# Gate pieces moved between groups, another order of products in a projection, and a last block gated before it is stored

## The chip, the core and the metric

The kernel runs on one core of one Trainium2 chip. Its engines are TensorE (PE in the profile, with PEld for its weight loads), VectorE (DVE), ScalarE (ACT), GpSimd (POOL) and SyncE (SP); transfers run on 16 DMA engines, issued by the queues of SP, POOL and ACT. The metric is the time of one execution on the device in microseconds, as the median of several runs.

## What is computed

One block of a diffusion model over 512 latent tokens and 256 context tokens with 2048 channels, all in fp32:

```python
shift, scale, gate = split(silu(c) @ w_ada + b_ada, 3)          # the same with c_ctx for the context
h  = rmsnorm(x, norm_g) * (1 + scale) + shift                   # hc for the context
p  = h @ w_in                                                   # q, k, v, z_a, u_b, z_b, g_a, g_b: 9216 columns
kc, vc = columns k, v of hc @ w_in
attn = attention(rope(rmsnorm(q)), [rope(rmsnorm(k)), rmsnorm(kc)], [v, vc])   # 12 query heads, 4 key heads
y_a = (attn * silu(z_a)) @ w_proj_a
y_b = (fft2(u_b).real * silu(z_b)) @ w_proj_b
y   = (sigmoid(g_a) * y_a + sigmoid(g_b) * y_b) @ w_out
out = rmsnorm(x + gate * y, final_g)
```

## The kernel before

**Products.** The large projections are computed in groups. A group makes a block of 512 tokens by 1024 or 512 columns with a Strassen-Winograd scheme in seven products, in the order P1, Q5, P2, Q6, P7, Q3, Q4 (`ONE_GROUP`), P1, P2, Q5, Q6, P7, Q3, Q4 (`OUT_GROUP`) for the branch and output projections. A product takes four pieces of weights (three in branch A), each 128x1024. A piece is multiplied in three passes (lines 322 to 324), since each fp32 factor is split into a high and a low part: ACT writes the high part of a piece (`whi`, line 173; `s` where it is split in halves), DVE the low part (`wlo`, line 174). PE needs both.

**Weights.** SP loads pieces in the order of use into a few raw buffers (`wr`, line 209), and a load waits until DVE has used what was in its buffer before. Some products need sums and differences of weight pieces. These are made in four chain tiles (`R`, numbers 1303 to 1306), which SP loads first, by accumulating loads on POOL's queue (line 277) or additions on DVE (line 256); P7's pieces are differences on DVE (line 262).

**Groups.** Groups 0 to 2 make the queries, 3 and 4 and later 6 and 7 the two gates g_a and g_b, and group 5 keys and values, for the context as well (`KV`). The modulated context is made from its rows beside groups 3 and 4. Then come 48 attention steps (12 heads in four blocks of queries), filled up with branch B's projection; then two groups of branch A's projection (10 and 11); then two groups of the output projection. `after(n, ...)` puts work off by n turns.

**The output gate.** `gate` is a product of one row with a matrix, and DVE makes it. The matrix comes in 32 pieces of 512 KB (`w_gate`), and `use_gate` (line 1091) multiplies each with half of the condition row (`crow`, loaded in two halves by `load_row`; `silu_of_row`, lines 1081 and 1082, turns a half into its silu in place) and sums it. `GATE_AT` tells behind which piece of which product a gate piece is used: 28 of them in the groups, the rest in the attention steps. A gate piece takes a raw buffer like a weight piece, from its load until DVE has used it.

**Merging.** Branch B's part of y is stored in `yb_d`. When a block of branch A's projection is finished, `branch_done` multiplies it with its gate on DVE (line 1357), adds `yb_d` to it by an accumulating transfer on POOL's queue (line 1359), and has it transposed by PE (line 1368) some turns later; the output projection's factors are made from the transposes.

Of the kernel before, what the change touches and what calls it, by code (L numbers as in the profile page):

```python
# [18 lines left out]
P = 128  # L19
# [38 lines left out]
OUT_GROUP = ("P1", "P2", "Q5", "Q6", "P7", "Q3", "Q4")  # L58

# [12 lines left out]
def context_piece(g, name, pc):  # L72
# [4 lines left out]
    if n % 6 == 0 and 18 <= n < 42:  # L77
# [39 lines left out]
def block_kernel(ctx, tc, xT, ctx_rows, ctx_toks, x, c_row, w_ss, w_gate, vecs, qkg, rope, dft_c, dft_s,  # L117
# [676 lines left out]
    class Group:  # L794
# [16 lines left out]
        def steps(self, name):  # L811
# [12 lines left out]
            for pc in range(self.pieces):  # L824
# [20 lines left out]
                if q is not None:  # L845
                    use_gate(q, get(("gate", q)))
                    if q == KK - 1:
                        raw_pools.append((rp, 1, "raw0", 1))
# [225 lines left out]
    def load_row(half):  # L1074
        row = crow[half] = rp.tile([P, 1024], F32, tag=f"raw{half}", bufs=1, name=uid("crow"))
# [47 lines left out]
    for g, kind in enumerate(KINDS):  # L1123
        if g == 3:
            jobs += [lambda: None] * 8 + [context_norm, lambda: None, lambda: None, context_spread]
# [11 lines left out]
        for name in ONE_GROUP:  # L1137
            if (g, name) in ((0, "Q4"), (KV + 1, "P1")):
                assert not any(p[2] == "raw0" for e in ahead for p, _ in e.raws) or g
# [3 lines left out]
            elif (g, name) == (KV + 1, "P2"):  # L1143
# [16 lines left out]
            elif (g, name) == (KV + 1, "Q6"):  # L1160
                raw_pools.append((gvp, 2, "raw", 2))
# [118 lines left out]
    def values(half):  # L1280
# [40 lines left out]
        if second and h == NH - 1:  # L1321
            branch_forms(2)
# [7 lines left out]
    def branch_forms(q):  # L1330
# [3 lines left out]
        branch_form("S3", q, u[:, :, lo])  # L1334
        nc.vector.tensor_tensor(u[:, :, hi], u[:, :, hi], v[:, :, hi], op=ALU.subtract)
        branch_form("Z5", q, u[:, :, hi])
        nc.vector.tensor_tensor(u[:, :, lo], u[:, :, lo], v[:, :, hi], op=ALU.add)
        branch_form("S2", q, u[:, :, lo])
        nc.vector.tensor_tensor(v[:, :, lo], v[:, :, lo], u[:, :, lo], op=ALU.subtract)
        give(u)  # L1340
        branch_form("S4", q, v[:, :, lo])
        give(v)
# [407 lines left out]
```

## Time and profile before

| | us |
|---|---|
| runs | 1353.55, 1360.97, 1353.3 |
| median | 1353.55 |
| the profiled execution | 1350.64 |
| its span on the core | 1348.6 |
| PE busy | 1296.9 |
| DVE busy | 995.4 |
| ACT busy | 683.5 |
| POOL busy | 179.5 |

The rows in the prediction are from this one profiled execution, so sums are made against 1350.64, and the median is 2.9 us above it. A row of stretches has the borders and length in us, then busy time and number of instructions of PE, PEld, DVE, ACT and POOL, the granted clock of PE as a share of full speed, the share of time in which the DMA engines were busy, and GB/s. A row of a timeline has its start and length, the engine and line, the operation, what it writes and reads, and in brackets how long the engine had been idle before it and what released it. A row of waits has the engine and line that waited, what it waited for, and the total, the number and the longest in us. Line numbers are those of the kernel before; the changed file's are larger by two in the first part and by seven further on.

### The profile page before, as it was taken

To read this page: it belongs to the slowest core of one execution; us is meant where nothing else is said; L and a number is where in the kernel's file an instruction comes from. 1 tells how busy PE (TensorE), PEld (TensorE's weight loads), DVE (VectorE), ACT (ScalarE), POOL (GpSimd) and SP (SyncE) were. 2 spreads that over 40 slices of the span, in tenths; PEclk is the share of its full clock that TensorE was granted. 3 is DMA by queue.
4 is the path that set the end of the run, shared out by engine and by line. 5 is a ranking of instruction groups with operands and counts; after the bars stand their busy time and mean duration, and the time that the engine had idled before them with its cause. 6 is when DMAs were issued, how large, how long until landed. Compare 5 with 4: busy or idle time off the path is not lost.

```text
span 1348.6 us, 17538 instructions
## 1 busy us (share of the span) xinstructions
PE 1296.9 (96%) x6522; PEld 1057.5 (78%) x6522; DVE 995.4 (74%) x1294; ACT 683.5 (51%) x1079; POOL 179.5 (13%) x244
## 2 busy tenths in 40 slices
PE   7999999999998999999989999889999999999997
PEld 3676888888886888888867877778888778878885
DVE  4666899889677778747567858667777767778776
ACT  5222655655454544444244534556677545555544
POOL 0110011111101011011021111111100202121210
PEclk9999999999998999999999999889999999999998
DMA  9898587888887999878669888965440799988986
GB/s 385 338 375 306 200 216 226 246 231 233 219 304 196 294 270 266 291 170 221 224 169 316 287 250 283 301 200 166 164 136 17 215 240 223 266 182 221 216 213 174
DMA packets 103718, 318.54 MB, mean 236 GB/s; under 512 B 9808, under 2 KB 33104, under 8 KB 99280
## 3 DMA queue, kind: packets, MB, share of 16 engines
q0 software_dynamic: 30288, 123.75, 38.8%
q1 hardware_dynamic: 48720, 163.65, 34.2%
q10 hardware_dynamic: 24624, 30.02, 6.4%
q8 instruction: 51, 0.84, 0.2%
q14 instruction: 35, 0.29, 0.1%
HBM read 283.30 MB, written 34.09 MB: 235 GB/s over the span
## 4 chain that ended last, share of the span: by engine, by line
PE 57%; DMA 15%; DVE 13%; issue 11%; ACT 4%; POOL 1%; ACTq 0%; DVEq 0%; SPq 0%; POOLq 0%
PE banks L322 8%; PE banks L324 7%; PE banks L323 7%; PE x L323 4%; PE x L324 4%; PE x L322 4%; DVE wlo L174 4%; DMA wr<-in_w_g 4%; PE y L323 4%; PE y L324 3%; PE y L322 3%; PE pd L521 2%; DVE s L174 2%; DMA cf_d<-qr 2%; PE pb L322 2%
## 5 line engine op out<-in xcount | busy, mean ns | idle before, releaser
L173 ACT ACTIVATE whi<-R 128x1024 fp32r<-128x1024 f32 x138 | 144.8, 1057 | 146.6 <-PE banks L324 48.9
L174 DVE TENSOR_TENSOR wlo<-R,whi 128x1024 fp32r<-128x1024 f32 x138 | 167.6, 1222 | 63.6 <-ACT whi L173 63.2
L173 ACT ACTIVATE whi<-wr 128x1024 fp32r<-128x1024 f32 (+1 forms) x123 | 128.4, 1050 | 138.3 <-PE banks L324 34.4
L174 DVE TENSOR_TENSOR wlo<-wr,whi 128x1024 fp32r<-128x1024 f32 (+1 forms) x123 | 148.8, 1214 | 57.8 <-ACT whi L173 57.4
L322 PE MATMUL banks<-whi,s 128*128 128x512 f32 x396 | 158.3, 400 | 7.2 <-DVE ev L849 5.8
L323 PE MATMUL banks<-wlo,s 128*128 128x512 f32 x396 | 156.6, 395 | 0.7 <-DVE wlo L174 0.7
L324 PE MATMUL banks<-whi,s 128*128 128x512 f32 x396 | 156.5, 395 | 0.0
L323 PE MATMUL x<-wlo,s 128*128 128x512 f32 x352 | 138.1, 392 | 4.9 <-DVE wlo L174 4.9
L324 PE MATMUL x<-whi,s 128*128 128x512 f32 x352 | 138.0, 392 | 0.0
L322 PE MATMUL x<-whi,s 128*128 128x512 f32 x352 | 137.9, 392 | 0.0
L323 PE MATMUL y<-wlo,s 128*128 128x512 f32 x316 | 123.2, 390 | 0.8 <-DVE wlo L174 0.8
L322 PE MATMUL y<-whi,s 128*128 128x512 f32 x316 | 123.2, 390 | 0.4 <-DVE cxe L992 0.4
L324 PE MATMUL y<-whi,s 128*128 128x512 f32 x316 | 122.8, 389 | 0.0
L277 POOL DMA_DIRECT2D R<-in_w_g x64 | 55.4, 866 | 451.1 <-DVE wlo L174 207.7
L173 ACT ACTIVATE s<-wr 128x512 fp32r<-128x512 f32 (+2 forms) x93 | 60.2, 676 | 66.6 <-DMA wr<-in_w_g 23.0
L322 PEld LDWEIGHTS banks<-whi,s 128*128 128x128 f32 x396 | 75.6, 191 | 23.3 <-issue 6.2
L324 PEld LDWEIGHTS banks<-whi,s 128*128 128x128 f32 x396 | 75.3, 190 | 15.8
L323 PEld LDWEIGHTS banks<-wlo,s 128*128 128x128 f32 x396 | 75.5, 191 | 15.6 <-DVE wlo L174 1.1
L174 DVE TENSOR_TENSOR s<-wr,s 128x512 fp32r<-128x512 f32 (+2 forms) x93 | 67.1, 752 | 23.3 <-ACT s L173 22.4
L323 PEld LDWEIGHTS x<-wlo,s 128*128 128x128 f32 x352 | 66.6, 189 | 19.1 <-DVE wlo L174 5.5
L324 PEld LDWEIGHTS x<-whi,s 128*128 128x128 f32 x352 | 66.7, 189 | 13.8
L322 PEld LDWEIGHTS x<-whi,s 128*128 128x128 f32 x352 | 66.5, 189 | 13.9
(288 smaller groups left out, 2846.2 us busy)
## 6 DMA issues: line engine op xcount, KB each, us to landing
wr<-in_w_g SPq DMA_DIRECT2D x128, 512.0 KB, 4.8
R<-in_w_g POOLq DMA_DIRECT2D x64, 512.0 KB, 6.9
wa<-in_w_ss POOLq DMA_DIRECT2D x26, 1024.0 KB, 8.2
R<-in_w_g SPq DMA_DIRECT2D x32, 512.0 KB, 5.3
wr<-in_w_gate SPq DMA_DIRECT2D x32, 512.0 KB, 4.9
wr<-in_w_o SPq DMA_DIRECT2D x24, 512.0 KB, 7.5
R<-in_w_o POOLq DMA_DIRECT2D x24, 512.0 KB, 8.3
wr<-in_w_pab SPq DMA_DIRECT2D x20, 512.0 KB, 5.4
```

The source lines that it names most:

```text
L173: first = nc.scalar.activation(hi, src, ACT.Copy)
L174: return first, nc.vector.tensor_tensor(lo, src, hi.bitcast(F32), op=ALU.subtract)
L277: nc.gpsimd.dma_start(chain[e.pc], e.nxt, accum_op=ALU.add)
L322: nc.tensor.matmul(o, ah, bh, start=start, stop=False, skip_group_check=cont)
L323: nc.tensor.matmul(o, ah, bl, start=False, stop=False, skip_group_check=cont)
L324: nc.tensor.matmul(o, al, bh, start=False, stop=stop, skip_group_check=cont)
L521: last = nc.tensor.matmul(acc[32 * j : 32 * j + 32, :256], c2[:, 8 * h + k, :], w[:, k, :], start=n < 4, stop=n >= KK - 4)
```

## The change

Several parts are changed together:

- **Gate pieces.** `GATE_AT` now has nine gate pieces in the K/V group (six before), five in group 6 and five in group 7 (six and eight before), and none in group 4 (one before). The six that are left are used in attention steps 8 to 33, every fifth step, where four were used in steps 4 to 22, every sixth.
- **The second half of the condition row** goes into the other buffer, `raw0`, is loaded earlier, and becomes silu one product earlier, at Q5 of group 6. The buffer `raw1` goes back to the weights in group 6 and `raw0` in the attention steps.
- **Context.** `context_norm` and `context_spread` stand two jobs later.
- **Branch A's products** come in the order P1, P2, Q5, P7, Q6, Q3, Q4, and the block that P7 finishes is finished at Q6.
- **Weight sums** of branch A are made in steps 8 to 25 (3 to 20 before).
- **Forms of branch A** (sums of blocks of its input, and their splits) are made one at a time in steps 43 to 49 instead of by fours at two steps and the end.
- **The last block** of branch A is gated in two parts. `less_gated` multiplies -Y by the gate and adds `yb_d` to it by the accumulating transfer before the last product, Q4; after Q4 `branch_done` multiplies the product with the gate and adds the two in SBUF, and has the block transposed after three turns instead of six.

```diff
+BRANCH_GROUP = ("P1", "P2", "Q5", "P7", "Q6", "Q3", "Q4")
...
-GATE_AT = ([(g, n, 1) for g in (1, 2) for n in ("P2", "Q6", "Q3")] + [(3, "Q5", 1), (4, "P2", 1)]
-           + [(5, n, 1) for n in ("P1", "P2", "Q6", "P7", "Q3", "Q4")] + [(6, n, 1) for n in ONE_GROUP if n != "Q5"]
-           + [(7, n, 1) for n in ONE_GROUP] + [(7, "Q6", 3)])
+GATE_AT = ([(g, n, 1) for g in (1, 2) for n in ("P2", "Q6", "Q3")] + [(3, "Q5", 1)]
+           + [(5, "P1", 1), (5, "Q5", 1), (5, "P2", 1), (5, "Q6", 1), (5, "P7", 1), (5, "P7", 3), (5, "Q3", 1),
+              (5, "Q3", 3), (5, "Q4", 0)] + [(6, n, 1) for n in ("P2", "Q6", "P7", "Q3", "Q4")]
+           + [(7, n, 1) for n in ("P1", "Q5", "P2", "Q6", "P7")])
...
-        for name in OUT_GROUP:
+        for name in BRANCH_GROUP:
             stream_product(name, BRANCH_A + n, BranchWeights(n), (), 3)
...
                 sub(self.Y, self.V, self.Y)
+                if self.g >= BRANCH_A:
+                    sub(self.V, self.V, self.acc["c"])
+                    self.done(1, 1, self.V, self.V)
+            elif name == "P7" and self.g >= BRANCH_A:
+                pass
...
+            elif name == "Q4" and self.g == BRANCH_A + 1:
+                self.done(1, 0, a, self.Y)
...
-        row = crow[half] = rp.tile([P, 1024], F32, tag=f"raw{half}", bufs=1, name=uid("crow"))
+        row = crow[half] = rp.tile([P, 1024], F32, tag="raw0", bufs=1, name=uid("crow"))
...
-            jobs += [lambda: None] * 8 + [context_norm, lambda: None, lambda: None, context_spread]
+            jobs += [lambda: None] * 10 + [context_norm, lambda: None, lambda: None, context_spread]
...
-            elif (g, name) == (KV + 1, "P2"):
+            elif (g, name) == (KV + 1, "Q5"):
                 silu_of_row(1, gvp.tile([P, 1024], F32, tag="raw", bufs=2, name=uid("e")))
...
-                raw_pools.append((gvp, 2, "raw", 2))
+                raw_pools += [(rp, 1, "raw1", 1), (gvp, 2, "raw", 2)]
...
+        if n and (half, c) == (1, 0):
+            nc.vector.tensor_tensor(w, v, w, op=ALU.mult)
+            nc.vector.tensor_tensor(t, t, w, op=ALU.add)
+            give(w)
+            merged[j, half] = t
+            after(3, lambda: turn_merged(j, half))
+            return
...
+    def less_gated(y, j):
+
+        nc.vector.scalar_tensor_tensor(y, y, -1.0, ga[1, j], op0=ALU.mult, op1=ALU.mult)
+        nc.gpsimd.dma_start(flat(y), yb_d[1, j], accum_op=ALU.add)
...
-        if 3 <= i < 21:
-            n, step = divmod(i - 3, 3)
+        if 8 <= i < 26:
+            n, step = divmod(i - 8, 3)
...
-        if 2 <= i < 26 and i % 6 in (2, 4):
-            n, last = NGATE + (i - 2) // 6, i % 6 == 4
+        if 5 <= i < 35 and i % 5 in (0, 3):
+            n, last = NGATE + (i - 5) // 5, i % 5 == 3
...
-        if i in (43, 47):
-            branch_forms(i > 43)
+        for q, name in {43: [(0, "Z5"), (0, "S3")], 44: [(0, "S2")], 45: [(0, "S4")], 47: [(1, "Z5")], 48: [(1, "S3")],
+                        49: [(1, "S2"), (1, "S4")]}.get(i, ()):
+            branch_forms(q, name)
...
+            if name == "Q6" and n:
+                load_ga(1, A_CHUNKS[n][0])
+            elif name == "Q3" and n:
+                after(1, lambda: less_gated(group.Y, A_CHUNKS[n][0]))
```

**ACT around the second half of the condition row**, in group 6. `qr` holds keys that line 966 stores into `k_d`; `e` is the helper of the row's silu and lies where `qr` lay; whi and s are high parts of weight pieces. Before:

```order
L966 DMA k_d<-qr 128x4x128 x2
L173 ACTIVATE whi_5472<-R_1306 128x1024
L173 ACTIVATE whi_5491<-wr_5489 128x1024
L173 ACTIVATE whi_5509<-wr_5507 128x1024
L1081 ACTIVATE e_5541<-crow_5386 128x1024
L173 ACTIVATE s_233<-wr_5544 128x2x256
L173 ACTIVATE s_346<-wr_5544 128x2x256
L857 COPY ev_5539<-y_5470 128x1024
```

Now (its lines 973, 175 and 1088 are those of 966, 173 and 1081):

```order
L175 ACTIVATE whi_5478<-R_1306 128x1024
L175 ACTIVATE whi_5497<-wr_5495 128x1024
L175 ACTIVATE whi_5515<-wr_5513 128x1024
L973 DMA k_d<-qr 128x4x128 x2
L175 ACTIVATE s_233<-wr_5547 128x2x256
L175 ACTIVATE s_346<-wr_5547 128x2x256
L1088 ACTIVATE e_5473<-crow_5392 128x1024
L175 ACTIVATE s_494<-wr_5565 128x2x256
L175 ACTIVATE s_610<-wr_5565 128x2x256
```

The store of the keys has moved behind three splits, and the splits of one more piece (two halves) have moved ahead of `e`.

**SP's loads from the end of the gate groups into the attention steps.** `in_w_g` are weights of the gates, `in_w_gate` pieces of the output gate, `k_d` and `v_d` keys and values, `b_d` tables of the Fourier mixing, `in_w_pab` weights of branches A and B. Before:

```order
L209 DMA wr_6296<-in_w_g 128x1024
L209 DMA wr_6367<-v_d 128x768
L209 DMA wr_6370<-in_w_gate 128x1024
L209 DMA wr_6403<-b_d 128x1024
L209 DMA wr_6416<-b_d 128x1024
L209 DMA wr_6426<-in_w_pab 128x1024
L209 DMA wr_6471<-k_d 128x768
L209 DMA wr_6523<-v_d 128x768
L209 DMA wr_6448<-in_w_pab 128x1024
```

Now:

```order
L211 DMA wr_6296<-k_d 128x768
L211 DMA wr_6449<-k_d 128x768
L211 DMA wr_6314<-v_d 128x768
L211 DMA wr_6379<-b_d 128x1024
L211 DMA wr_6400<-b_d 128x1024
L211 DMA wr_6413<-in_w_pab 128x1024
L211 DMA wr_6423<-in_w_pab 128x1024
L211 DMA wr_6517<-v_d 128x768
```

The gate piece is gone, and the second piece of branch B's weights stands directly behind the first, ahead of the second load of values; the second load of keys has moved ahead.

**DVE at P7 of the last gate group.** Line 262 (264 now) makes the difference of a chain tile and a loaded piece, line 1091 (1098 now) uses a gate piece. Before:

```order
L262 TENSOR_TENSOR wr_6165<-R_1304,wr_6165 128x1024
L174 TENSOR_TENSOR wlo_6168<-R_1305,whi_6167 128x1024
L174 TENSOR_TENSOR wlo_6186<-R_1306,whi_6185 128x1024
L1091 TENSOR_SCALAR wr_6091,gparts<-wr_6091,crow_5386 128x1024
L174 TENSOR_TENSOR wlo_6208<-wr_6148,whi_6207 128x1024
L262 TENSOR_TENSOR wr_6204<-R_1306,wr_6204 128x1024
L174 TENSOR_TENSOR s_234<-wr_6165,s_233 128x2x256
```

Now, some ten instructions earlier:

```order
L1098 TENSOR_SCALAR wr_5935,gparts<-wr_5935,crow_5392 128x1024
L264 TENSOR_TENSOR wr_6204<-R_1306,wr_6204 128x1024
L176 TENSOR_TENSOR wlo_6065<-wr_6000,whi_6064 128x1024
L176 TENSOR_TENSOR wlo_6097<-wr_6055,whi_6096 128x1024
L264 TENSOR_TENSOR wr_6133<-R_1303,wr_6133 128x1024
```

The difference with chain tile 1306, the last one before, has become the first of the four.

More of the change, by code (lines that the diff above doesn't have):

```diff
@@ L1138, in block_kernel @@
             if (g, name) in ((0, "Q4"), (KV + 1, "P1")):
-                assert not any(p[2] == "raw0" for e in ahead for p, _ in e.raws) or g
+                assert not any(p[2] == "raw0" for e in ahead for p, _ in e.raws)
                 load_row(int(g > 0))
@@ L1321, in values @@
         if second and h == NH - 1:
-            branch_forms(2)
+            for name in FORM_ORDER:
+                branch_forms(2, name)
     def branch_form(name, q, src):
@@ L1483, in block_kernel @@
     for n, group in enumerate(a_groups):
[L1484 to L1485 removed]
+        for name in BRANCH_GROUP[1 - n :]:
+            if name == "Q6" and n:
+                load_ga(1, A_CHUNKS[n][0])
+            elif name == "Q3" and n:
+                after(1, lambda: less_gated(group.Y, A_CHUNKS[n][0]))
+            elif name == "Q5":
                 load_ga(0, A_CHUNKS[n][1])
```

31 lines of the change are left out of this document (16 added, 15 removed).

## The prediction

> **What bounds the kernel now.** I read the page's engine and clock rows first, then the table of stretches, then the rows on which TensorE (PE) starts again after an idle time, and last what each of those waited for.
>
> ```profile
> PE 1296.9 (96%) x6522; PEld 1057.5 (78%) x6522; DVE 995.4 (74%) x1294; ACT 683.5 (51%) x1079; POOL 179.5 (13%) x244
> ...
> PEclk9999999999998999999999999889999999999998
> ```
>
> PE is busy 96% of the span, and the change takes no matmul away. So only two things can be won: PE's idle time, and stretches in which it was busy at a lower clock (the 8s).
>
> ```profile
> 420.00:440.00 20.00, 15.12 (x59) 12.05 (x58) 13.23 (x17) 8.97 (x13) 2.07 (x3) 0.83 0.69 194
> 440.00:540.00 100.00, 100.00 (x443) 82.79 (x442) 76.55 (x119) 49.48 (x72) 8.20 (x10) 1.00 0.93 280
> ...
> 700.00:720.00 20.00, 14.80 (x54) 11.36 (x53) 12.33 (x16) 10.24 (x15) 0.90 (x2) 0.83 0.85 268
> ...
> 800.00:820.00 20.00, 17.10 (x70) 13.71 (x69) 12.28 (x16) 4.10 (x5) 0.86 (x1) 0.91 0.74 200
> ...
> 840.00:860.00 20.00, 13.81 (x58) 11.04 (x57) 9.47 (x14) 8.20 (x12) 1.96 (x3) 0.83 1.02 354
> ...
> 880.00:900.00 20.00, 16.51 (x105) 14.63 (x104) 13.93 (x22) 11.59 (x22) 3.03 (x5) 0.86 0.66 191
> ...
> 1180.00:1200.00 20.00, 17.96 (x82) 14.61 (x81) 12.48 (x11) 11.14 (x12) 3.92 (x5) 0.91 0.98 224
> ```
>
> The stretch 440 to 540 is the undisturbed rate: 443 matmuls in 100 us, 0.226 each, so 20 us hold 88.6. PE's restarts inside the other stretches, and one outside them (the sixth, after which the clock stayed), are called A to G:
>
> ```profile
> 428.80 0.80 PE L323 MATMUL x<-wlo,s 128*128 128x512 f32 x1 [4.88 <-DVE wlo L174]
> ...
> 707.75 0.80 PE L322 MATMUL x<-s,s 128*128 128x512 f32 x1 [4.65 <-ACT s L173]
> ...
> 809.61 0.79 PE L323 MATMUL x<-s,s 128*128 128x512 f32 x1 [2.90 <-DVE s L174]
> ...
> 848.01 0.77 PE L322 MATMUL banks<-whi,s 128*128 128x512 f32 x1 [5.83 <-DVE ev L849]
> ...
> 895.84 0.69 PE L1111 MATMUL banks<-ident,wr 128*128 128x128 f32 x2 [3.28 <-DVE ptl L174]
> ...
> 1082.96 1.09 PE L1368 MATMUL banks<-ident,s 128*128 128x128 f32 x8 [2.21 <-DMA s<-yb_d]
> ...
> 1194.42 1.50 PE L1368 MATMUL banks<-ident,s 128*128 128x128 f32 x8 [2.04 <-ACT whi L173]
> ```
>
> What follows an idle time, after A:
>
> ```profile
> 427.00:430.40 3.40, 1.60 (x4) 1.31 (x5) 3.07 (x6) 0.00 (x0) 0.00 (x0) 0.50 0.28 64
> 430.40:433.80 3.40, 3.40 (x10) 2.63 (x9) 3.40 (x5) 0.00 (x0) 0.00 (x0) 0.51 0.86 286
> ```
>
> PE works at half speed for some microseconds after it starts again, so a stall costs more than its idle time. What a stall is worth, in whole: in A, B and C, where all matmuls are alike, counted: (88.6-59)x0.226 = 6.7 us, (88.6-54)x0.226 = 7.8, (88.6-70)x0.226 = 4.2. Idle time plus the missing clock share of 20 us gives 4.9+3.4 = 8.3, 5.2+3.4 = 8.6 and 2.9+1.8 = 4.7; the counts are 0.81 to 0.91 of that. With 0.87 the stretches of mixed sizes give D (6.2+3.4)x0.87 = 8.3, E (3.5+2.8)x0.87 = 5.5, G (2.0+1.8)x0.87 = 3.3. F is its 2.2. B to G together are 31.3 us, the most that the change can take from these places.
>
> The Trainium skill ("TensorE: Matmul & The Clock Gate", What's actually happening) says that the clock is halved after an idle window of about 3.4 us. The trace differs: idle times of 2.90 and 2.04 us brought it here. By that rule what I leave of B below, an idle time shorter than that, would cost no clock, and the forecast would be some 1.5 us lower; the rows decide.
>
> **The change, part by part.** *A stays.* The VectorE (DVE) rows around it are in the same order in both kernels, and the wait there is for a store of earlier work:
>
> ```profile
> DVE qr L1040 <- DMA qz_d<-qr: 6.8, 1, 6.8
> ```
>
> *B, the second half of the condition row.* ScalarE (ACT) stores keys and then stands in line 1081 until they have landed, with the split of the next weight piece behind it:
>
> ```profile
> 690.75 1.05 ACTq L966 DMA_DIRECT2D k_d<-qr  x2
> ...
> 706.12 1.06 ACT L1081 ACTIVATE e<-crow 128x1024 f32<-128x1024 f32 x1 [10.67 <-DMA k_d<-qr]
> ```
>
> and line 966's transfers:
>
> ```profile
> DMA to landing us min/median/max: 2.9/4.1/14.9
> ```
>
> In the changed order three weight splits come ahead of the store (so it goes out about 1.9 us later, 692.6), and both halves of one more weight piece ahead of line 1081. PE can then run one piece further: 12 matmuls, 2.7 us, from 703 to 705.7. If the store again takes 14.9 us it lands at 707.5; then come e (1.06), the row's product on DVE (1.2) and the split of the next piece (0.7), and PE goes on at 710.4 after 4.7 us idle, worth (4.7+3.4)x0.87 = 7.0. If it lands within 10 us, nothing is left. So the gain is 0.8 to 7.8; the long landing is the nearest row, line 966's median the farthest, and the condition row's own load no longer runs just ahead of it: I take the middle, 4.0.
>
> *C, last gate group.* The last load of product P7 waits until a gate piece has been used and its buffer is free:
>
> ```profile
> 796.85 1.22 DVE L1091 SCALAR_TENSOR_TENSOR wr<-wr,crow 128x1024 f32<-128x1024 f32 x1
> ...
> 807.72 1.22 DVE L262 TENSOR_TENSOR wr<-R,wr 128x1024 f32<-128x1024 f32 x1 [8.51 <-DMA wr<-in_w_g]
> ```
>
> ```profile
> 798.11 1.71 SPq L209 DMA_DIRECT2D wr<-in_w_g  x2
> ```
>
> With fewer gate pieces in this group that load takes the buffer that the gate before it frees, 5.8 us earlier; PE's 2.90 go. But the four differences now begin with chain tile 4, ahead of two splits, and its accumulating load is the last of four:
>
> ```profile
> 770.15 0.88 POOL L277 DMA_DIRECT2D R<-in_w_g  x1 [0.34 <-DVE s L174]
> ```
>
> ```profile
> 779.14 1.23 DVE L262 TENSOR_TENSOR wr<-R,wr 128x1024 f32<-128x1024 f32 x1 [7.98 <-DMA R<-in_w_g]
> ```
>
> DVE waited until 779 for tile 3; tile 4, issued 1.2 us later, may land at 780 to 784, and the splits behind it are late by 0 to 3. Gain 1.2 to 4.2; I take 2.5.
>
> *D and E, the first attention steps.* Here ACT waits for weights of branch B, in two places:
>
> ```profile
> ACT whi L173 <- DMA wr<-in_w_pab: 9.0, 2, 6.3
> ```
>
> ```profile
> ACT whi L173 <- DMA wr<-in_w_pab: 3.7, 1, 3.7
> ```
>
> ```profile
> 833.37 7.68 SPq L209 DMA_DIRECT2D wr<-in_w_pab  x3
> ```
>
> ```profile
> 884.07 1.21 DVE L1091 SCALAR_TENSOR_TENSOR wr<-wr,crow 128x1024 f32<-128x1024 f32 x1
> ```
>
> ```profile
> 884.11 1.53 SPq L209 DMA_DIRECT2D wr<-in_w_pab  x2
> ```
>
> For D the gate piece just ahead and its load are gone, and the two branch weights stand together behind the Fourier tables in SyncE's (SP) order, so the second goes out 8 to 10 us before 833. That covers 5.8 of idle: I take 7.5 of 8.3 (5 to 8.3; a value-row load moved ahead of them could eat 2 to 3). For E the load waited for a gate's buffer (884.07+1.21 = 885.28); now its buffer is free some 45 us before it is needed: 5.5 (3 to 5.5).
>
> *F.* The first merged block is transposed three weight pieces later, behind P7 instead of Q6: 36x0.226 = 8.1 us, against 2.2 of waiting for the accumulating store: gain 2.2 (1 to 2.2).
>
> *G, the last merged block.* Before, line 1359's store stands between the product and the transposes:
>
> ```profile
> 1184.19 0.85 POOL L1359 DMA_DIRECT2D s<-yb_d  x1 [0.28 <-DVE s L1357]
> ```
>
> ```profile
> DMA to landing us min/median/max: 5.3/7.2/12.0
> ```
>
> Now the store comes before Q4, and an addition of 1.2 us takes its place. What is late next is the split of the first output weights on ACT (the releaser that the row 1194.42 names). Gain 0 to 3.3; I take 2.5.
>
> *What is added.* Nine instead of six gate pieces in the K/V group, and six instead of four in the attention steps:
>
> ```profile
> L1091 DVE SCALAR_TENSOR_TENSOR wr<-wr,crow x32: 1206/1221/1226, 272.5 to 948.7; 128x1024 f32<-128x1024 f32 x32
> ```
>
> ```profile
> wr<-in_w_gate SPq DMA_DIRECT2D x32, 512.0 KB, 4.9
> ```
>
> ```profile
> 540.00:700.00 160.00, 158.78 (x698) 130.34 (x698) 107.05 (x118) 67.26 (x115) 17.89 (x21) 1.00 0.76 217
> ...
> 900.00:1040.00 140.00, 139.90 (x932) 122.33 (x931) 105.86 (x173) 92.77 (x182) 13.46 (x22) 1.00 0.42 133
> ```
>
> K/V group: 3x1.22 = 3.7 us of DVE and three loads, against 53 us in which DVE is free and DMA engines free a quarter of the time. Hidden: 0; with one load late, 3.7+4.9 = 8.6. I take 1. Attention: 2x1.22 = 2.4, against 34 us free, but three pieces come close together and score rows queue behind them: 0 to 2.4+4.9 = 7.3; I take 2. The weight sums, five steps later, lie where POOL works 13 us of 140. The forms are the same instructions in smaller lots, the one at the end of the attention spread ahead: 0, at most 1.
>
> Sum: 4.0+2.5+7.5+5.5+2.2+2.5 = 24.2, less 3.0 is 21.2. The profiled execution took 1350.64 us, so 1329.4; the median of the runs lies 2.9 above it, which gives 1332 us.
>
> **The rivals.** *The waits move.* If B's store again lands late (gain 0.8) and, in the attention steps, two of the six gates stop DVE as E did (2x5.5), then 24.2-3.2-11-3 = 7 is left: 1347 us. For it: buffers stay few, and every late load in B to E was one that waited for a buffer. Against: DMA is busy only 0.42 there.
>
> *The change does not do what it says in B and G.* Line 1081 still waits for the same store, and the row 1194.42 names a split, not the store. Then 24.2-3.2-2.5-3 = 15.5 are won: 1338 us.
>
> *Slower.* In the K/V group each gate that lands after its turn on DVE holds up the split behind it, as A's wait does, at 6.7 each. It decides from a landing 3 us late on. Six of nine: 40 us, so 1350.6-24.2+40+2+2.9 = 1371. For it: nine gates, one SP queue in order, and each holding a buffer. Against: PE idles 1.2 of 160 us there now, and DVE has a third free.
>
> **How the numbers follow.** Forecast 0.65 (its own range 1322, everything of B to G, to 1340), waits move 0.17, B and G unchanged 0.10, slower 0.08. About 1% can be told from no change here: 13.5 us, so below 1340 is faster. The forecast and half of the third case make 0.70 faster, the second and the other half 0.22 within 1%, the last 0.08. The range reaches from 1320 (with the smallest stalls gone too) to 1352, a little over the second case; it leaves out the slower one and the worst sums of the added costs.
>
> **What would show it.** Right: stalls at 424 with its half clock unchanged, the rows of half clock near 850, 898 and 1196 gone, line 1081 waiting less than 5 us, line 1368 with no wait for a store. Wrong: a new idle time above 2 us at a gate of the K/V group or at line 1091 in attention, line 1081 waiting over 10 us again, or more stretches of half clock than three.

## The result, and the profile after

The changed kernel took 1342.89 us in the median of seven runs (1341.84 to 1347.56), the kernel before 1353.55 in the median of seven beside them (1351.98 to 1360.97). The ratio is 0.9919 with a 95% interval of 0.9896 to 0.9941. Faster by 10.7 us, or 0.8%: within the range and on the forecast's side, but half of the 21.2 us forecast, and less than the 1% that was called a difference.

The engine rows of the page (the profiled execution took 1343.44 us, its span 1341.6):

```profile
PE 1290.6 (96%) x6522; PEld 1052.7 (78%) x6522; DVE 995.6 (74%) x1295; ACT 682.2 (51%) x1079; POOL 180.6 (13%) x244
...
PEclk9999999999999999999998999999999999999999
```

The same matmuls are there, and the slices of lower clock went from four to one. The table of stretches, columns as before:

```profile
420.00:440.00 20.00, 16.54 (x73) 13.12 (x72) 15.20 (x19) 8.50 (x10) 3.46 (x4) 1.00 0.68 198
...
500.00:520.00 20.00, 17.64 (x71) 14.43 (x72) 15.61 (x26) 9.71 (x15) 1.73 (x2) 0.91 0.87 287
520.00:700.00 180.00, 179.19 (x791) 148.00 (x790) 124.96 (x141) 75.73 (x127) 21.48 (x24) 1.00 0.79 228
700.00:720.00 20.00, 14.98 (x53) 11.56 (x52) 10.30 (x14) 7.45 (x12) 0.12 (x1) 0.83 0.71 224
...
780.00:800.00 20.00, 16.85 (x67) 13.46 (x66) 11.65 (x13) 7.31 (x10) 1.69 (x2) 0.91 0.73 218
840.00:860.00 20.00, 15.09 (x68) 12.19 (x67) 11.22 (x16) 9.50 (x14) 1.96 (x3) 0.91 0.90 327
```

Against 88.6 matmuls in an undisturbed stretch of equal ones, 502, 711 and 789 still or newly lack 18, 36 and 22. PE's restarts in its timeline say what was waited for:

```profile
502.36 0.50 PE L325 MATMUL y<-s,s 128*128 128x512 f32 x1 [4.39 <-DVE s L176]
...
710.61 0.50 PE L324 MATMUL x<-s,s 128*128 128x512 f32 x1 [4.18 <-ACT s L175]
...
788.96 0.50 PE L325 MATMUL x<-wlo,s 128*128 128x512 f32 x1 [3.15 <-DVE wlo L176]
...
844.98 0.47 PE L324 MATMUL banks<-whi,s 128*128 128x512 f32 x1 [1.47 <-DVE ev L849]
...
853.51 0.50 PE L324 MATMUL banks<-whi,s 128*128 128x512 f32 x1 [3.44 <-DVE R L1229]
...
946.58 0.39 PE L324 MATMUL banks<-s,s 128*128 128x256 f32 x1 [1.29 <-DVE ptl L176]
...
1093.27 0.47 PE L324 MATMUL banks<-whi,s 128*128 128x512 f32 x1 [1.41 <-DVE s L849]
...
1156.20 0.47 PE L324 MATMUL banks<-whi,s 128*128 128x512 f32 x1 [1.41 <-DVE s L849]
```

E (896), F (1083) and G (1194) are gone, and D's idle time (845) is 1.47 us for 5.83. B (711) and C (789) are there. New are the waits at 502, at 853, at 946, and the pair at 1093 and 1156.

Both kernels issue the same number of matmuls, so the distance between them at any place is the start of the n-th matmul in one trace less its start in the other. From place to place that distance changed by, in us (minus is won):

| stretch (times of the kernel before) | forecast | measured |
|---|---|---|
| to 440 (A) | 0 | -4.4 |
| 440 to 514 (context) | none | +6.1 |
| 514 to 727 (K/V group and B) | -3.0 | -0.8 |
| 727 to 814 (C) | -2.5 | +0.5 |
| 814 to 903 (D, E and the first attention gates) | -13.0, +2 for the gates | -8.8 |
| 903 to 956 (a later gate) | in these +2 | +1.5 |
| 956 to 1098 (F) | -2.2 | -2.7 |
| 1098 to 1190 (products of the output) | 0 | +4.9 |
| 1190 to the end (G) | -2.5 | -3.3 |

A value can be off by 0.2 us or so, by which matmul stands at a border. The column adds up to -7.0, for 7.2 between the two profiled executions. Without A, whose rows are the same in both kernels, the stretches gained 15.6 and lost 13.0. A's idle time varied with no edit near it: 2.5 to 5.2 us in the runs below that load the same bytes. So one pair of traces tells where time went, and the medians by how much.

### The profile page after: what moved, and what is told of

The parts are those of the page before. It is cut to its first block, busy times and chain, and to the rows that moved or that the text cites. A ratio compares the mean times of both kernels' runs of the same rounds, so it can differ in the third digit from the quotient of the medians.

```text
span 1341.6 us, 17565 instructions
## 1 busy us (share of the span) xinstructions
PE 1290.6 (96%) x6522; PEld 1052.7 (78%) x6522; DVE 995.6 (74%) x1295; ACT 682.2 (51%) x1079; POOL 180.6 (13%) x244
## 4 chain that ended last, share of the span: by engine, by line
PE 75%; DMA 10%; DVE 8%; ACT 3%; issue 2%; POOL 0%; SPq 0%; ACTq 0%; DVEq 0%; POOLq 0%
PE banks L324 10%; PE banks L325 10%; PE banks L326 10%; PE x L325 6%; PE x L326 6%; PE x L324 6%; PE y L325 5%; PE y L324 5%; PE y L326 5%; DVE wlo L176 3%; PE banks L1280 2%; PE pd L523 2%; DMA wr<-in_w_g 2%; PE pb L324 2%; DMA R<-in_w_g 2%
## 5 line engine op out<-in xcount | busy, mean ns | idle before, releaser
L325 PEld LDWEIGHTS banks<-wlo,s 128*128 128x128 f32 x396 | 74.4, 188 | 16.8 <-DVE wlo L176 2.8
L325 PEld LDWEIGHTS x<-wlo,s 128*128 128x128 f32 x352 | 66.4, 189 | 21.2 <-DVE wlo L176 7.5
L324 PEld LDWEIGHTS x<-whi,s 128*128 128x128 f32 x352 | 66.5, 189 | 13.8
L326 PEld LDWEIGHTS x<-whi,s 128*128 128x128 f32 x352 | 66.5, 189 | 13.8
```

Of the source, the lines that this page charges most:

```text
L324: nc.tensor.matmul(o, ah, bh, start=start, stop=False, skip_group_check=cont)
L325: nc.tensor.matmul(o, ah, bl, start=False, stop=False, skip_group_check=cont)
L326: nc.tensor.matmul(o, al, bh, start=False, stop=stop, skip_group_check=cont)
```

## The experiments

Each edit is to the changed kernel unless said otherwise, and each ratio is to runs of the kernel before that were made beside it, with its 95% interval. The changed kernel's interval is 0.9896 to 0.9941. Only those of runs 3, 5 and 8 lie wholly below it; all others overlap it. So differences in us between the medians of other runs and the changed kernel are given as they came out, and aren't clear of noise; what such a run shows of a cause, it shows by its trace.

**1. Context two jobs earlier again**

```diff
-            jobs += [lambda: None] * 10 + [context_norm, lambda: None, lambda: None, context_spread]
+            jobs += [lambda: None] * 8 + [context_norm, lambda: None, lambda: None, context_spread]
```

> The changed kernel with the context's row scales back at their old place (eight empty jobs instead of ten ahead of them); all else as changed. Theory: the new idle time of 4.39 us at 502 of the changed kernel comes from DVE's order: with ten jobs, line 1062 (waiting 7.5 us for the store of context rows) stands ahead of two half-splits that PE needs; with eight it stands behind them, as before. Then the idle time at 502 is gone although line 1062 still waits 7 to 8 us, and the kernel takes 5 to 6 us less than the changed one (about 1337, 0.988 of before). Rival: DMA is 0.86 busy there and PE would soon wait for the next weights anyway: the idle time moves by some us and the time stays within 2 us of 1343.

1343.48 us (0.9917, 0.9888 to 0.9946): no gain. What stood at 502 in the changed kernel, from DVE's timeline:

```profile
501.22 0.48 DVE L1062 SCALAR_TENSOR_TENSOR qr<-wr,gain,qr 128x256 f32<-128x256 f32 x1 [7.48 <-DMA cf_d<-qr]
501.62 1.28 DVE L176 TENSOR_TENSOR s<-R,s 128x512 fp32r<-128x512 f32 x2
```

and the same rows with this edit, then its stretches:

```profile
493.82 1.28 DVE L176 TENSOR_TENSOR s<-R,s 128x512 fp32r<-128x512 f32 x2
502.23 0.88 DVE L1062 SCALAR_TENSOR_TENSOR qr<-wr,gain,qr 128x256 f32<-128x256 f32 x2 [7.12 <-DMA cf_d<-qr]
```

```profile
500.00:520.00 20.00, 19.84 (x88) 16.08 (x88) 12.67 (x22) 8.58 (x13) 0.00 (x0) 1.00 0.88 269
700.00:720.00 20.00, 19.38 (x84) 15.26 (x83) 14.32 (x18) 10.10 (x13) 2.58 (x3) 1.00 0.79 241
780.00:800.00 20.00, 15.10 (x56) 12.29 (x57) 11.68 (x13) 6.18 (x8) 1.75 (x2) 0.83 0.69 195
```

DVE waits as long for the same store, but PE doesn't (88 matmuls): the two half-splits `s<-R,s`, which PE needs, now stand ahead of the waiting row, in the changed kernel behind it. The 4.39 us are the most of any profile: with the changed order (the changed kernel and runs 2, 4, 6, 7, 9 and 10) PE idled 1.41 to 4.39 us here, with the old one (the kernel before and runs 1, 3, 5, 8 and 11) 0 to 1.38. Unasked, B went too (84 instead of 53), since the keys' store landed after 5.7 us. The matmuls then ran 9.2 us ahead of the changed kernel at 728, 6.2 at 785, 3.4 at 801, 1.2 at 1052, and 0.0 at the end. Small waits at 736 to 741 took most of the first part, and this the next:

```profile
784.90 0.79 PE L325 MATMUL x<-wlo,s 128*128 128x512 f32 x1 [5.30 <-DVE wlo L176]
```

**2. C's difference back in the chain's order**

```diff
-DIFF_IN_LINE = (4, 6, 8, 9)
+DIFF_IN_LINE = (4, 6, 7, 8, 9)
```

> The changed kernel with the differences of P7 in the last gate group put into line (each behind the split of two pieces before) instead of where the scheduler puts them. Theory: at 789 PE idles 3.15 us because the difference with chain tile 1306 stands first on DVE and waits 11.1 us for the last of four accumulating loads, with two splits behind it. In line it waits behind them: no idle time at 789, and about 4 us less than the changed kernel (1339). Rival: the load of P7's last piece, which waits for a gate's buffer, is as late as before (wait of 8.5 us, idle 2.9 at about 805), and takes its place: no gain, 1342 to 1344.

1334.83 us (0.9879, 0.9825 to 0.9933), 8.1 below the changed kernel. In the profiled executions, 8.1 apart too, 3.0 of this lie ahead of the edit's place (at 502 the wait was shorter, with no edit there) and 4.9 at C. Its stretch at C:

```profile
780.00:800.00 20.00, 20.00 (x90) 16.58 (x89) 16.51 (x20) 11.32 (x15) 3.09 (x4) 1.00 1.04 323
```

C is gone, 90 matmuls against 67, and it is gone in every profile with this edit (runs 2, 3, 5 and 8); in all the others of the changed gates PE idles 1.37 to 5.30 us here. It was made by these two rows of the changed kernel, an accumulating load on POOL and the difference on DVE that waits for it:

```profile
772.61 0.88 POOL L279 DMA_DIRECT2D R<-in_w_g  x1 [0.34 <-DVE s L176]
```

```profile
786.54 1.23 DVE L264 TENSOR_TENSOR wr<-R,wr 128x1024 f32<-128x1024 f32 x1 [11.12 <-DMA R<-in_w_g]
```

**3. Both**

```diff
-DIFF_IN_LINE = (4, 6, 8, 9)
+DIFF_IN_LINE = (4, 6, 7, 8, 9)
...
-            jobs += [lambda: None] * 10 + [context_norm, lambda: None, lambda: None, context_spread]
+            jobs += [lambda: None] * 8 + [context_norm, lambda: None, lambda: None, context_spread]
```

> The changed kernel with both edits: the context's rows at their old place and the differences of P7 in the last gate group in line. The first alone won 5.6 us at 502 and 7.4 at 711 and gave them back at 785, where PE idled 5.30 instead of 3.15; the second alone won 5 us. Theory: what is given back at 785 is only the wait for the accumulating load of chain tile 1306, which stands at a fixed time of the DMA queues; with the differences in line it is not waited for, and both gains are kept: 1329 to 1332, no idle time over 2 us between 500 and 830. Rival: the weights of the last gate groups as a whole come no faster (DMA 0.92 to 0.95 busy): the gain of the first edit is lost again at another load before 830, and the time stays at 1335, that of the second alone.

1333.10 us (0.9832, 0.9786 to 0.9878). That is 1.7 below the second alone by the medians, 6.4 by the ratios, whose intervals overlap; the profiled executions are 1.7 apart, though this one lost 4.3 more at A, so 6.0 without A. Its stretches:

```profile
500.00:520.00 20.00, 20.00 (x90) 16.56 (x89) 10.97 (x21) 7.94 (x13) 0.00 (x0) 1.00 0.93 276
700.00:720.00 20.00, 14.92 (x56) 11.50 (x55) 10.55 (x13) 8.12 (x11) 0.82 (x1) 0.83 0.67 213
780.00:800.00 20.00, 20.00 (x90) 16.55 (x89) 15.75 (x19) 10.47 (x15) 2.61 (x3) 1.00 1.03 311
```

502 and C are gone together, B is back: PE idle 4.53 us there, with a landing of 16.8. So the context's place alone doesn't take B away.

**4. e in another buffer.** The silu's helper no longer lies where the stored keys lay; it takes the gate pieces' other buffer.

```diff
-                silu_of_row(1, gvp.tile([P, 1024], F32, tag="raw", bufs=2, name=uid("e")))
+                silu_of_row(1, rp.tile([P, 1024], F32, tag="raw1", bufs=1, name=uid("e")))
...
             elif (g, name) == (KV + 1, "Q6"):
-                raw_pools += [(rp, 1, "raw1", 1), (gvp, 2, "raw", 2)]
+                raw_pools.append((rp, 1, "raw1", 1))
+            elif (g, name) == (KV + 1, "Q3"):
+                raw_pools.append((gvp, 2, "raw", 2))
```

> The changed kernel with the helper of the row's silu (e) in the free raw buffer instead of where the keys lie that are being stored, and the two buffers of that region given to the weights two products later (Q3 instead of Q6). Theory: PE's idle time at 711 (4.18 and 0.84) comes from e's wait of 9.0 us for the store of the keys, with the split of the next piece behind it on ACT. Without that wait it goes, worth 7 us with the half clock (1336). Rival: the weights themselves are late there (two buffers fewer for two products, the store of 1024 small packets beside them): PE then idles 3 us or more within the next 20 us and the time stays within 2 us of 1343.

1345.35 us (0.9932, 0.9905 to 0.9958). Nothing waits for that store now, and B is longer. Its timeline and waits:

```profile
712.50 0.80 PE L324 MATMUL x<-s,s 128*128 128x512 f32 x1 [6.21 <-ACT s L175]
```

```profile
ACT s L175 <- DMA wr<-in_w_g: 11.9, 2, 6.2
```

ACT now waits for the weights themselves. As the edit also leaves the weights one raw buffer fewer for a while and gives two others back later, it doesn't tell whether they would be late without it.

**5. Keys stored early,** with 1 and 2. The second half's keys aren't stored; the first half's are stored twice instead, some 70 us earlier.

```diff
-            nc.scalar.dma_start(by_group((v_d if c else k_d)[:, :, 2 * half + b, :]), r[:, b])
+            if c or not half:
+                nc.scalar.dma_start(by_group((v_d if c else k_d)[:, :, 2 * half + b, :]), r[:, b])
+            if not c and not half:
+                nc.scalar.dma_start(by_group(k_d[:, :, 2 + b, :]), r[:, b])
```

> The kernel of the two edits (context's rows back, differences of P7 in line), but the second half's keys are not stored at 691: in their place the first half's are stored twice, some 70 us earlier (the attention then runs on wrong keys, with as much work). Over all profiles PE's idle time near 711 went with the landing of that store: 4.2 to 4.7 us where it took 16.5 to 16.9 us, 1.5 where it took 10.6, 0.4 where it took 5.7. Theory: line 1088 and the region's buffers wait for this store alone, and nothing else in that stretch is late: the idle time of 4.53 and 0.55 at 711 goes, and the kernel takes 6 to 7 us less than the two edits' (1326 to 1328). Rival: the weights of the next pieces are late as well (as with the helper in another buffer, where PE idled 6.21): 2 us or more of idle time stay at 705 to 730, or come at the next P7, and the gain is under 3 us (1330 or more).

1334.82 us (0.986, 0.9836 to 0.9884), no less than run 3. Its timeline and waits at B:

```profile
707.16 0.50 PE L324 MATMUL x<-s,s 128*128 128x512 f32 x1 [2.09 <-ACT s L175]
```

```profile
ACT s L175 <- DMA wr<-in_w_g: 11.3, 2, 7.9
```

Without the store the idle time halves, from 4.53, and a wait for weights takes over. B has two waits, one behind the other.

**6. Fewer gate bytes.** The gate pieces in the groups load 256 of their 1024 columns, and DVE makes three quarters of the product from them; the rest is left out.

```diff
...
-                    stream(("gate", q), w_gate[q], 1024, 1, "raw")
+                    stream(("gate", q), w_gate[q][:, :256], 1024, 1, "raw")
...
```

> The changed kernel, but of every gate piece in the groups only a quarter of the columns is loaded (128 KB instead of 512), and three quarters of the product are computed from it; 9.8 of 318 MB less. Buffers, queues and the order of instructions stay, but for a few on DVE near 400 us. Theory (bytes): the loads of groups 6 and 7 share a DMA time that is 0.92 to 0.95 used; with fewer bytes the idle times at 711 and 789 shrink to under half, and the kernel takes 8 us or more less than the changed one (1335 or less). Rival (order): these waits are set by what stands where in the queues (a store with small packets, accumulating loads, buffers that come free late), and fewer bytes take off less than a third: 1340 to 1344.

1338.09 us (0.9887, 0.9851 to 0.9923), 4.8 below the changed kernel. Its restarts at B, at C and at a later wait:

```profile
705.39 0.49 PE L324 MATMUL x<-s,s 128*128 128x512 f32 x1 [1.49 <-ACT s L175]
...
782.42 0.79 PE L325 MATMUL x<-wlo,s 128*128 128x512 f32 x1 [3.27 <-DVE wlo L176]
...
801.65 0.58 PE L325 MATMUL y<-wlo,s 128*128 128x512 f32 x1 [2.58 <-DVE wlo L176]
```

B's idle time shrinks with the traffic (so does A's, to 0.82 us); C's doesn't, and DVE waits 11.49 us for the accumulating load, for 11.12. The last row comes from a wait of 7.09 us on DVE for a plain load of weights; in the changed kernel that wait was 4.22, and PE didn't feel it. So by this one trace the bytes are part of B and not of C. The verdict is mixed, since DVE's work per gate fell by 0.3 us as well.

**7. Attention gates three steps later**

```diff
-        if 5 <= i < 35 and i % 5 in (0, 3):
-            n, last = NGATE + (i - 5) // 5, i % 5 == 3
+        if 8 <= i < 38 and i % 5 in (3, 1):
+            n, last = NGATE + (i - 8) // 5, i % 5 == 1
```

> The changed kernel with its six gate pieces of the attention asked for and used three steps later (steps 8 to 36). Theory: PE's idle time of 3.44 us at 853 comes from the first of them: DVE waits 4.8 us for its load and stands ahead of the first score maximum. Three steps later it stands behind it: the idle time at 853 goes, worth 4 us (1339). Rival: what is late there is the first attention step's own work (keys, values, first fill), so PE idles about as long with the gate away, within 1.5 us of the changed kernel; or the gates stop DVE at a later place by as much.

1339.02 us (0.9896, 0.9862 to 0.9931). What was waited for at 853 in the changed kernel, and this kernel's stretch:

```profile
850.75 1.23 DVE L1098 SCALAR_TENSOR_TENSOR wr<-wr,crow 128x1024 f32<-128x1024 f32 x1 [4.79 <-DMA wr<-in_w_gate]
```

```profile
840.00:860.00 20.00, 18.53 (x95) 15.26 (x95) 13.56 (x18) 13.62 (x21) 1.94 (x3) 1.00 0.86 319
```

The first gate's load was late for DVE, and the score rows that PE needs stood behind it. Three steps later the gate costs nothing there (95 matmuls for 68); of all the profiles of the changed gates, only this one and run 8's have no stall there (0.88 to 5.83 us in the others). But F came back in the profiled execution, and took most of it:

```profile
1082.03 1.97 PE L1394 MATMUL banks<-ident,s 128*128 128x128 f32 x8 [3.42 <-DMA s<-yb_d]
```

**8. Runs 1, 2 and 7 together**

```diff
-DIFF_IN_LINE = (4, 6, 8, 9)
+DIFF_IN_LINE = (4, 6, 7, 8, 9)
...
+            jobs += [lambda: None] * 8 + [context_norm, lambda: None, lambda: None, context_spread]
...
+        if 8 <= i < 38 and i % 5 in (3, 1):
+            n, last = NGATE + (i - 8) // 5, i % 5 == 1
```

> The two edits and the gate pieces of the attention three steps later. Alone, the last removed the 3.44 us at 853 but 3.42 us came at 1082 (the first merged block's transposes waiting for its accumulating store). Theory: all three together take 1326 to 1330, with the idle time at 1082 of 3 us as the one that was not there before. Rival: the gain at 853 is given back whole at 1082, and the time is that of the two edits alone, within 1.5 us.

1331.22 us (0.9829, 0.9791 to 0.9867): the fastest, 22 us below the kernel before, and only 1.9 below run 3. Its gain over run 3 lies within both intervals. The stall at 853 is gone, and F is back here too:

```profile
1070.75 1.09 PE L1394 MATMUL banks<-ident,s 128*128 128x128 f32 x8 [2.49 <-DMA s<-yb_d]
```

**9. The projection as before.** Order of the products, where blocks are finished, and the last block, all undone; the gates stay.

```diff
-        for name in BRANCH_GROUP:
+        for name in OUT_GROUP:
...
-                if self.g >= BRANCH_A:
-                    sub(self.V, self.V, self.acc["c"])
-                    self.done(1, 1, self.V, self.V)
-            elif name == "P7" and self.g >= BRANCH_A:
-                pass
...
-            elif name == "Q4" and self.g == BRANCH_A + 1:
-                self.done(1, 0, a, self.Y)
...
-            if name == "Q6" and n:
-                load_ga(1, A_CHUNKS[n][0])
-            elif name == "Q3" and n:
-                after(1, lambda: less_gated(group.Y, A_CHUNKS[n][0]))
```

> The changed kernel with the whole part on branch A's projection undone: products in the old order, P7's block finished at P7, last block gated and stored after Q4. Theory: that part wins 2.2 at the first merged block and 3.3 at the last, and loses as much at four new idle times (1.41 at 1093, 1.41 at 1156, 1.28 at 1166, 0.76 at 1177), so it is worth nothing: within 2 us of the changed kernel (1341 to 1345), with the old idle times near 1075 and 1187 back and the four gone. Rival: the part is worth what the prediction gave it, 4.7 us: 1347 to 1348.

1347.88 us (0.9961, 0.9921 to 1.0001), 5.0 above the changed kernel. Both waits for the merged blocks are back:

```profile
1074.84 1.09 PE L1380 MATMUL banks<-ident,s 128*128 128x128 f32 x8 [2.26 <-DMA s<-yb_d]
...
1191.96 1.94 PE L1380 MATMUL banks<-ident,s 128*128 128x128 f32 x8 [4.44 <-DMA s<-yb_d]
```

The waits of 1.41 at 1093 and 1156 are gone with the new order; they stand in every profile that has this order, and in none that hasn't. By the medians this part is worth 5.0 after paying for them, which speaks against the theory that it was worth nothing; the intervals overlap.

**10. Only the last block as before,** with the new order kept.

```diff
-            elif name == "Q4" and self.g == BRANCH_A + 1:
-                self.done(1, 0, a, self.Y)
...
-        if n and (half, c) == (1, 0):
-            nc.vector.tensor_tensor(w, v, w, op=ALU.mult)
-            nc.vector.tensor_tensor(t, t, w, op=ALU.add)
...
-            if name == "Q6" and n:
-                load_ga(1, A_CHUNKS[n][0])
-            elif name == "Q3" and n:
-                after(1, lambda: less_gated(group.Y, A_CHUNKS[n][0]))
```

> The changed kernel with only the last block as before: not gated before Q4, stored by the accumulating transfer after it, transposed after six turns; the new order of products stays. With the whole part on the projection undone the time rose by 5 us, and in that profile PE idled 2.26 at 1075 and 4.44 at 1192. Theory: most of it is the last block: 3.5 to 5 us more than the changed kernel (1346 to 1348), an idle time of 3 us or more near 1185 with the accumulating store as its releaser. Rival: the order of products brings the most, and the last block alone, whose transposes also wait for a split, is worth under 2 us (1345 or less).

1348.39 us (0.9948, 0.992 to 0.9975), 5.5 above the changed kernel. The profiled execution, one of the quicker ones at 1342.94, has no wait at G. Its wait for a merged block stands 20 us earlier:

```profile
1173.36 1.92 PE L1385 MATMUL banks<-ident,s 128*128 128x128 f32 x8 [2.26 <-DMA s<-yb_d]
```

By the medians all of run 9's 5.0 us would belong to the last block. But the intervals overlap, this run's times reach from 1338.96 to 1351.38, and its profiled execution is 0.5 us quicker than the changed kernel's. So what the last block is worth alone, and which wait costs it, is open.

**11. The kernel before, with the gate part alone:** `GATE_AT`, the condition row's buffer and silu, and the attention steps as in the changed kernel, all else as before. Against the kernel before:

```diff
+GATE_AT = ([(g, n, 1) for g in (1, 2) for n in ("P2", "Q6", "Q3")] + [(3, "Q5", 1)]
+           + [(5, "P1", 1), (5, "Q5", 1), (5, "P2", 1), (5, "Q6", 1), (5, "P7", 1), (5, "P7", 3), (5, "Q3", 1),
+              (5, "Q3", 3), (5, "Q4", 0)] + [(6, n, 1) for n in ("P2", "Q6", "P7", "Q3", "Q4")]
+           + [(7, n, 1) for n in ("P1", "Q5", "P2", "Q6", "P7")])
...
+        row = crow[half] = rp.tile([P, 1024], F32, tag="raw0", bufs=1, name=uid("crow"))
...
+            elif (g, name) == (KV + 1, "Q5"):
...
+        if 5 <= i < 35 and i % 5 in (0, 3):
+            n, last = NGATE + (i - 5) // 5, i % 5 == 3
```

> The kernel before with the change's gate part alone: the new table of gate pieces, the six in the attention steps, the condition row's second half in the other buffer and one product earlier. Context, branch A's products, last block, weight sums and forms as before. Theory (the parts add up): the projection part was worth 5 us (1347.9 without it against 1342.9), the context part nothing (1343.5 without it), so the gate part alone takes 1347 to 1349, with the idle times at 842 and 892 of before cut to one of 3 to 4 at about 850, and that at 807 replaced by one of 3 to 5 at about 787. Rival: the parts need each other (what one wins ahead of a late transfer is given back at it): the gate part alone is within 2 us of the kernel before, or worth over 8 us.

1346.23 us (0.9946, 0.9918 to 0.9974), 7.3 below the kernel before by the ratio (0.0054 of 1353.55). With the projection's 5.0 (run 9) that makes 12.3, for the whole change's 10.7. So, as far as medians tell, these two parts account for it; the weight sums and the forms were not run alone. E is gone (0.70 us idle at 891), and D's wait is 1.47 (at 843). B (4.49) and C (3.40) are there, and so is the stall of 853, behind a wait of 7.17 us on DVE for the first gate of the attention:

```profile
854.38 0.80 PE L323 MATMUL banks<-whi,s 128*128 128x512 f32 x1 [5.83 <-DVE R L1221]
```

## Why the prediction was right, and where its steps failed

The sign and the range held because three of the six stalls (E, F and G) went for about their price, and no gate of the K/V group cost anything. The forecast's size, and its own range up to 1340, failed on the steps below. By the prediction's own yardstick, 13.5 us, the time came out within 1% of the kernel before, a case that it gave 0.22 for 0.70 to faster.

There is luck in the total. In the two traces, the context and the products of the output cost 11.0 us for which the sum had no term, and A gave 4.4 that the change didn't make. Two of the signs that the prediction had named as wrong were seen: PE idled 3.44 us behind a gate on DVE in the attention (853), and four stretches have a lowered clock (502, 711, 789 and 853) where more than three was the sign. Line 1081 (now 1088) waited 8.96 us, between the two limits set for it.

**A** stayed, with 3.46 us of idle time for 4.88, but without the half clock that was to remain. The 4.4 us of the table were not the change's (the last section tells where the clock's part comes from).

**B, mis-sized at the end of its bound.** The store went out later, as forecast (692.0 for 690.75), but it took 16.5 us, even more than the 14.9 of before. The landings of the two stores' line in the changed kernel, in run 1 and in run 6:

```profile
DMA to landing us min/median/max: 5.2/5.6/16.5
```

```profile
DMA to landing us min/median/max: 3.4/4.9/5.7
```

```profile
DMA to landing us min/median/max: 3.3/4.7/10.6
```

The idle time followed the longest landing: 4.18, 0.40 and 1.49 us. I took the middle of the bound (4.0), against the only row there was for this place; its own lower end, 0.8, was near the truth (0.0 to 0.8). The line that still waits is the one named:

```profile
708.98 1.06 ACT L1088 ACTIVATE e<-crow 128x1024 f32<-128x1024 f32 x1 [8.96 <-DMA k_d<-qr]
```

The rival on B held in this. But what it left out, runs 4 and 5 showed: behind the store a wait for weights is ready to take over.

**C, mis-sized.** The wait for the load that a gate's buffer held up fell from 8.51 to 4.22 us on DVE, and PE no longer felt it. The risk was named, the accumulating load of chain tile 1306. It was given 780 to 784 and landed at 786.5 (772.61 + 13.9). I had priced it with the wait for the tile ahead of it, though it is the last of four. Gain 2.5 became a loss of 0.5, and in run 2's trace one number took the stall away, 4.9 us.

**D, the mechanism right, its cost elsewhere.** The loads of branch weights went out earlier, and the idle time there fell from 5.83 to 1.47. What gates cost in the attention, which I spread over it as 2 us for the added ones, came as one stall: the first gate's load was late (4.79 on DVE) with score rows behind it, 3.44 us of idle and the clock. Run 7 shows it by its absence. This gate isn't an added one. In the kernel before, DVE waited at the same place for the first attention gate's load, and PE didn't stop for it:

```profile
853.27 1.23 DVE L1091 SCALAR_TENSOR_TENSOR wr<-wr,crow 128x1024 f32<-128x1024 f32 x1 [2.85 <-DMA wr<-in_w_gate]
```

So part of what D gave was taken by the wait that stood next.

**E, F and G** came as worked out in size, 6.5, 2.7 and 3.3 for 5.5, 2.2 and 2.5. F's and G's waits came back with the old order (run 9), E stayed away with the gate part alone (run 11).

**The K/V group's nine gates** were priced at 1 and cost nothing (179.19 us busy of 180). The slower rival fell with that.

**Context, the step that was missing.** The prediction has no term for the two jobs of delay. They moved a row with a 7 us wait ahead of two half-splits on DVE, and PE stood still for 4.39: 6.1 us, the largest single loss of this trace. The order of DVE's rows shows it without any time; the prediction compares it at A alone. By medians the step's worth is open: undoing it alone gained nothing (run 1).

**The new order of products** was counted for F and G alone. PE now waits twice 1.41 us for DVE's row at line 849, and 1.28 and 0.76 us for splits; 4.9 us in all. So in the two traces the order and the last block together won only 1.1 us (2.7 and 3.3 less 4.9); the 5.0 of run 9 is by medians.

**The rival that the waits move** held in part. What it named came: B's store landed late again, and two gates of the attention stopped DVE (4.79 us at 851, 1.76 at 944), at less than its price of 5.5 each, 3.44 and 1.29 us of idle. Beside it stands what it didn't name, transfers that move less than the work ahead of them. Run 1 won 9.2 us by 728 and had lost 5.8 of them by 801, most plainly at the difference that waits for tile 1306, where DVE waited 13.16 instead of 11.12 (the load, issued 5.3 us earlier, landed 4.1 earlier); the rest went later. With C's order mended, the same edit kept what it won (run 3, no stall at 780, 1.7 to 6.4 us under run 2, within the intervals). What gave F back in runs 7 and 8 is in their traces: the accumulating transfer of `yb_d` that the first merged block waits for landed 18.1 and 17.2 us after its issue, against 9.6 in the changed kernel and 9.2 to 9.8 in runs 1 to 6. Why it took so long there is open.

## What to carry to other kernels

Where an engine's rows run in order, a wait costs PE anything from nothing to most of its length, by what stands behind it (DVE's wait of 7.1 to 8.4 us at 502 cost PE 0 to 4.4): before a job is moved by two turns, read which rows change sides with each waiting row. Price a transfer on which a gain rests by the longest landing seen at its own place, not by the median of its line, and an accumulating load by its place in its chain. Run 1's gain, ahead of a transfer that moved less, came to nothing, and in run 3, with that transfer's wait moved, it stayed: so mend the last stall of a stretch first.

## What was not expected of the hardware

**One store, 5.7 to 16.9 us.** The same two keys' transfers, 256 KB each, landed after 14.9 us in the kernel before, 16.5 in the changed one, 16.7 to 16.9 in runs 2, 3, 7, 8 and 11, 13.8 in run 4, 10.6 with fewer gate bytes, and 5.7 in run 1. The Trainium skill ("DMA: Bandwidth & Descriptors", Queues, rings and completion order) says that a DMA engine takes the queues that have work in turn, a packet at a time. The traces agree. The store is 1056 small packets, 0.52 MB. In the changed kernel they moved at 36 a us from 698 to 704, while SP's loads (0.68 MB) and the accumulating loads (0.82 MB) moved beside them, and at 184 a us from 706 to 708.6, when the accumulating loads were over. In run 1, which loads as much, all of them moved between 694.6 and 696.7, a gap in which SP's loads moved 0.04 MB and the accumulating loads 0.11. So the store is quick where its packets meet a gap in the other queues. Why run 1 has the gap there stays open.

**The clock after an idle time.** In the changed kernel 3.46 us of idle at 426 left it whole, and 4.39 at 502 brought it to 0.60:

```profile
426.30:429.70 3.40, 3.40 (x15) 2.80 (x16) 3.40 (x6) 0.58 (x1) 0.00 (x0) 1.00 0.72 192
502.30:505.70 3.40, 3.34 (x9) 2.68 (x10) 3.40 (x7) 0.23 (x1) 0.86 (x1) 0.60 0.70 165
```

In run 2 the idle time at 501 was only 2.17 us, and what followed ran slower still:

```profile
501.40:504.80 3.40, 3.40 (x11) 2.65 (x10) 3.40 (x7) 0.00 (x0) 0.86 (x1) 0.56 0.66 121
```

So the length of the idle time alone doesn't decide. Its place does, as all thirteen profiles together show. Their clock changes only on a grid of 3.41 us, to half or to full (in the kernel before half from 426.9 to 433.7, in the changed one from 503.0 to 506.4). Of the grid's steps at full clock, 51 had PE idle for 1.9 us or more, by the matmul rows, and each of them was followed by half clock; of the 2751 with 1.65 us or less, none was; of the nine between, two were. The 3.46 us at 426 lay across a border of the grid, 1.67 us on one side and 1.79 on the other. The 2.17 us of run 2 lay within one step. So where a stall lies on this grid decides whether it costs its clock too, and no edit here set that: that A lost its half clock was luck. A's idle time was only 1.42 us shorter than before (3.46 for 4.88); the rest of its 4.4 us is the clock that stayed.
